# A gate folded into a projection's weights, and the work around the last tile's norm reordered

## The chip, the cores and the metric

The kernel runs on one core of one Trainium2 chip. The metric is the device time of one execution in microseconds (us); of several runs the median counts.

## The reference

One layer of a streaming encoder over 1024 positions and 1024 channels, in float32. Only the middle matters here: two branches (a gated DeltaNet and a banded attention) are each projected and merged by gates; the merged rows go through an output projection, are multiplied by a gate per channel and added to the residual, and are normalised. A second sub-layer follows.

```python
gate_a, gate_b = jnp.split(jax.nn.sigmoid(gates + b_gate[l]), N_BRANCHES, axis=-1)
merged = gate_a * (o_a @ w_branch_a[l]) + gate_b * (o_b @ w_branch_b[l])
mix = merged @ w_o[l]
x = layernorm(DEEPNORM_ALPHA * x + gate_t * mix, ln1_g[l], ln1_b[l])

h = x * (1.0 + scale_f) + shift_f
u = causal_dwconv(h @ w_up[l], conv_ffn[l]) + b_conv_ffn[l]
u_gate, u_val = jnp.split(u, 2, axis=-1)
ffn = (jax.nn.silu(u_gate) * u_val) @ w_down[l]
x = layernorm(DEEPNORM_ALPHA * x + gate_f * ffn, ln2_g[l], ln2_b[l])
```

`gate_t` is a row of 1024 numbers that depends on the conditioning vector alone.

## The kernel before

Every matrix is split into a high and a low part (`split`, L178 and L181: a cast that makes the high part, then a subtraction that makes the low part), and each product is made of three matmuls: high by high, high by low, low by high. The matmuls take 128x512 at a time.

Four stages meet at the place in question. The **branch projections** (`pbr`, L1043) make the merged rows `mh` (high) and `ml` (low; `hh` and `hl` in the profile's names), 128 channels at a time. During the second branch the eight row blocks of `w_o` (k0 to k7) are loaded through the buffers `raw` (three of them) and split into `wo`.

The **output projection** is `mix(t)` (`pwo`, L1107) for eight tiles t of 128 positions, two halves of 512 channels each. For each tile VectorE multiplies the result by the gate row `gtb` (L1135), adds ALPHA times the residual row `r` (L1137 and L1139), and takes statistics (L1081 to L1084); GpSimd raises the variance to the power -1/2 (L1085), VectorE multiplies once more (L1090), and ScalarE normalises (L1093). `store_x1` (L1143, L1144) multiplies the normalised row by `g1b`, adds `b1b`, both on GpSimd for all tiles but one, and writes the row to memory. Eight transposes (`pn`, L1156) turn the tile, and ScalarE applies scale and shift (L1159), out of PSUM.

The **Up stage** (`pup`, L1282) works in a Strassen-like form with seven products for a pair of weight columns. Its operands over positions are blocks: T1 is the difference of the second four tiles and the first four (L1163, then a split), T2 a difference of the halves of the channels (`t2f`, L1170), T3 and T4 further sums (`build`; L1210, L1211, L1215, L1216). Its operands over weights are sums of blocks of `wr` (S1 to S4, L1244, L1247, L1265, L1268), split into `wop`. The first products need only tiles 0 to 3 or the first weights; the others need what comes out of the last tile, t = 7.

The order on each engine is decided by a scheduler when the kernel is built. Each engine then works strictly through its own list, waiting for semaphores; loads and stores stand in one list of the load queue (SP). `tc.issue_after(x)` keeps the scheduler from placing an instruction ahead of x. In the kernel before, all builds of T2 to T4 are held behind `last`, the low half of the last tile's split, and behind the power of the last norm; the store of tile 6 is made with `late`, as is that of tile 7.

Of the kernel before, what the change touches and what calls it, by code (L numbers as in the profile page):

```python
# [154 lines left out]
def hybrid_layer(  # L155
# [873 lines left out]

    wo = []  # L1030
    for br in range(2):
# [4 lines left out]
        for j in range(NK):  # L1036
# [24 lines left out]
            if br == 1 and (j % 2 == 1 or j == NK - 1):  # L1061

                for k in ([j // 2] if j < NK - 1 else range(3, NK)):
                    at_ = MA[2 * k:2 * k + 2] if k < 4 else OB[2 * k - 8:2 * k - 6]
                    a, b = (place(o, [P, D], F32R, "wo") for o in at_)
                    load_split(a, b, w_o2[k * P:k * P + P, :], ACT, DVE)
# [3 lines left out]
    def bcast(key, src):  # L1070
        t_ = ring(key, [P, D])
        SP.dma_start(t_, src.partition_broadcast(P).rearrange("p o n -> p (o n)"))
        return t_
# [53 lines left out]
    for t in range(NT):  # L1127
# [4 lines left out]
        m_ = ring("x1", [P, D])  # L1132
        for n in range(2):
            N = slice(512 * n, 512 * n + 512)
            DVE.tensor_tensor(m_[:, N], ps[n], gtb[:, N], ALU.mult)  # L1135
            if t >= MS:
                DVE.scalar_tensor_tensor(r[:, N], r[:, N], ALPHA, m_[:, N], ALU.mult, ALU.add)  # L1137
        if t < MS:
            DVE.scalar_tensor_tensor(r, r, ALPHA, m_, ALU.mult, ALU.add)  # L1139
        norm(r, r, [slice(0, 512), slice(512, 1024)] if t >= MS else [slice(0, 1024)])  # L1140

        def store_x1(t=t, r=r, m_=m_):
            POOL.tensor_tensor(m_, r, g1b, ALU.mult)  # L1143
            (DVE if t in X1D else POOL).tensor_tensor(m_, m_, b1b, ALU.add)  # L1144
# [2 lines left out]
        if t < X1L:
# [1 line left out]
        else:
            late.append(store_x1)  # L1150
# [425 lines left out]
```

## Time and profile before

| | us |
|---|---|
| median of three runs | 2240.79 |
| lowest, highest | 2235.49, 2244.45 |
| profiled execution | 2240.64 |
| its span | 2238.9 |

The span is the time from the first to the last instruction of the profiled execution. All times of rows are counted from the span's start. In a timeline each row has its start, its duration, engine, line, operation, what is written from what, and in brackets the idle time of the engine just before with the instruction that ended it. The granted clock is the share of full speed that TensorE was given.

### The profile page before, as it was taken

How to read it: one execution, taken by the hardware profiler on the slowest of the kernel's cores; microseconds unless marked ns; L12 is line 12 of the kernel's file. 1: busy time of each engine (PE TensorE's matmuls, PEld its weight loads, DVE VectorE, ACT ScalarE, POOL GpSimd, SP SyncE). 2: the span in 40 equal slices, each digit the busy share in tenths (PEclk: the TensorE clock that was granted, in tenths of full speed). 3: DMA queues.
4: the chain of work that ended last, by engine and by line, in shares of the span. 5: the costliest groups of instructions: out<-in, count | busy, mean ns of one | idle time of the engine just before them, and what ended most of it. 6: DMA issues, size and time to landing. Idle time of an engine off the chain costs nothing.

```text
span 2238.9 us, 31612 instructions
## 1 busy us (share of the span) xinstructions
PE 2129.2 (95%) x11469; PEld 1782.0 (80%) x11469; DVE 1585.5 (71%) x3233; ACT 1025.3 (46%) x2193; POOL 617.0 (28%) x558
## 2 busy tenths in 40 slices
PE   6998999999999999999999999999899999999987
PEld 5687787777878787798989788887688888888875
DVE  8568575765758754567775643458898888889998
ACT  4645243433424334567765642224554444445532
POOL 4323232322323322233432423334110000000064
PEclk9999999999999999999999999999999999999998
DMA  9232333423242412211211523332222222253213
GB/s 284 84 111 73 90 101 105 120 65 117 74 123 80 125 33 98 68 54 47 80 46 59 167 85 128 108 132 94 66 94 85 85 85 85 85 207 110 106 48 131
DMA packets 227263, 220.48 MB, mean 98 GB/s; under 512 B 27354, under 2 KB 184467, under 8 KB 227107
## 3 DMA queue, kind: packets, MB, share of 16 engines
q1 hardware_dynamic: 227027, 218.44, 30.8%
q8 instruction: 90, 1.47, 0.3%
q14 instruction: 66, 0.54, 0.1%
q10 hardware_dynamic: 80, 0.03, 0.0%
HBM read 177.48 MB, written 47.23 MB: 100 GB/s over the span
## 4 chain that ended last, share of the span: by engine, by line
PE 45%; DVE 5%; issue 1%; ACT 1%; POOL 1%; DMA 0%; DVEq 0%; SPq 0%; ACTq 0%; POOLq 0%
PE pup L1282 18%; PE pbr L1043 8%; PE pdn L1460 7%; PE pwo L1107 3%; PE pqk L885 2%; PE pv L900 2%; PE po L975 2%; PE pp L960 1%; PE ps L934 1%; PE pdn L1506 1%; DVE dop L181 0%; DVE hh L1526 0%; DVE hl L181 0%; DMA raw<-in_w_branch_a_dram 0%; DVE G L1163 0%
## 5 line engine op out<-in xcount | busy, mean ns | idle before, releaser
L181 POOL TENSOR_TENSOR wl<-raw,wh 128x1024 fp32r<-128x1024 f32 x88 | 211.4, 2405 | 327.5 <-ACT wh L178 297.9
L1282 PE MATMUL pup<-hh,wop 128*128 128x512 f32 x704 | 229.4, 397 | 5.8 <-ACT SB L1295 3.9
L1282 PE MATMUL pup<-t,wop 128*128 128x512 f32 x792 | 189.9, 393 | 3.9 <-DVE t L181 2.5
L1282 PEld LDWEIGHTS pup<-t,wop 128*128 128x128 f32 x792 | 148.8, 188 | 37.7 <-DVE t L181 2.8
L1282 PEld LDWEIGHTS pup<-hh,wop 128*128 128x128 f32 x704 | 135.0, 192 | 35.4 <-ACT SB L1295 4.3
L178 ACT CAST wh<-raw 128x1024 fp32r<-128x1024 f32 x88 | 92.4, 1050 | 140.1 <-DMA raw<-in_w_in_dram 57.2
L285 PE MATMUL pqkv<-hh,wh 128*128 128x512 f32 x352 | 143.0, 407 | 0.0
L1323 POOL TENSOR_TENSOR cc<-cc,G 128x512 f32<-128x512 f32 x22 | 36.8, 1670 | 378.5 <-DVE G L1305 329.2
L1282 PE MATMUL pup<-hl,wop 128*128 128x512 f32 x352 | 139.9, 398 | 0.9 <-DVE hl L181 0.9
L285 PE MATMUL pqkv<-hl,wh 128*128 128x512 f32 x352 | 140.7, 400 | 0.0
L285 PE MATMUL pqkv<-hh,wl 128*128 128x512 f32 x352 | 139.6, 398 | 0.0
L664 DVE TENSOR_TENSOR FT<-FT,G 128x16 f32<-128x16 f32 (+30 forms) x248 | 120.9, 488 | 19.5 <-POOL G L609 12.2
L178 ACT CAST wop<-wr 128x512 fp32r<-128x512 f32 x110 | 67.1, 621 | 119.7 <-DVE wr L1268 66.5
L945 POOL TENSOR_SCALAR G<-G,FT 128x640 f32<-128x640 f32 (+4 forms) x103 | 69.9, 680 | 183.0 <-DVE FT L944 162.0
L181 DVE TENSOR_TENSOR wop<-wr,wop 128x512 fp32r<-128x512 f32 x110 | 79.5, 731 | 26.2 <-ACT wop L178 25.8
L285 PE MATMUL pgt<-hh,wl 128*128 128x512 f32 x240 | 95.2, 397 | 0.8 <-POOL wl L181 0.8
L285 PE MATMUL pgt<-hh,wh 128*128 128x512 f32 x240 | 95.5, 398 | 0.2 <-DVE tmp L531 0.2
L285 PE MATMUL pgt<-hl,wh 128*128 128x512 f32 x240 | 94.8, 395 | 0.0
L964 DVE TENSOR_TENSOR pl<-pp,ph 128x512 fp32r<-128x512 f32 (+2 forms) x116 | 72.5, 635 | 17.4 <-ACT ph L963 16.6
L1460 PE MATMUL pdn<-hl 128*128 128x512 f32 x324 | 78.0, 394 | 6.1 <-DVE hh L1474 6.1
L1342 DVE SCALAR_TENSOR_TENSOR G<-cc,vt,G 128x1023 f32<-128x1023 f32 (+1 forms) x58 | 75.0, 1297 | 8.1 <-ACT G L1339 8.1
L942 ACT ACTIVATE G<-G,FT 128x640 f32<-128x640 f32 (+4 forms) x103 | 71.6, 695 | 18.9 <-DVE FT L937 16.9
(446 smaller groups left out, 6160.1 us busy)
## 6 DMA issues: line engine op xcount, KB each, us to landing
raw<-in_w_in_dram SPq DMA_DIRECT2D x72, 512.0 KB
wr<-in_w_up_dram SPq DMA_DIRECT2D x44, 512.0 KB
raw<-in_w_ada_dram SPq DMA_DIRECT2D x32, 512.0 KB
dr<-g_d SPq DMA_DIRECT2D x18, 512.0 KB
dr<-in_w_down_dram SPq DMA_DIRECT2D x18, 512.0 KB
wa<-in_w_ada_dram SPq DMA_DIRECT2D x32, 256.0 KB
gates_d<-GT SPq DMA_DIRECT2D x32, 256.0 KB
g_d<-G SPq DMA_DIRECT2D x15, 512.0 KB
```

Source lines behind the costliest of these rows:

```text
L178: ACT.copy(h, src)
L181: return le.tensor_tensor(l, src, f(h), ALU.subtract).ins
L285: PE.matmul(ps, a[:, k, :], r[k][:, 512 * n:512 * n + 512], start=(k == 0 and a is wh and r is rh), stop=(k == NK - 1 and a is wl))
L664: DVE.tensor_tensor(pr[:, :, 0:i + 1], ft[:, :, 0:i + 1], fa[:, i:i + 1, 0:i + 1].to_broadcast([P, 8, i + 1]), ALU.mult)
L942: ACT.activation(sb[:, 0:n], sb[:, 0:n], AF.Exp, bias=mx[:, nb - 1:nb], scale=-1.0, accum_out=mx[:, 2:3])
L945: POOL.tensor_scalar(sb[:, 0:n], sb[:, 0:n], mx[:, 3:4], 0.0, ALU.mult, ALU.add)
L964: DVE.tensor_tensor(pl[:, B, :], pp, f(ph[:, B, :]), ALU.subtract)
L1043: PE.matmul(ps, a[:, k, :], r[k][:, N], start=(k == 0 and a is w[0] and r is rh), stop=(k == NK - 1 and a is w[1]))
L1107: PE.matmul(ps[n], a[:, t, k, :], wo[k][b][:, 512 * n:512 * n + 512], start=(k == 0 and a is mh and b == 0), stop=(k == NK - 1 and a is ml))
L1282: PE.matmul(ps, a[:, u, k, :], b[v][k], start=(new and k == 0 and u == 0 and v == 0), stop=(k == 3 and u == 1), skip_group_check=not new)
L1342: DVE.scalar_tensor_tensor(y[:, d:], cc[:, :S - d], col("conv_f", tap * 44 + ti), y[:, d:], ALU.mult, ALU.add)
L1460: PE.matmul(sets[s_][i], a[:, u, i * P:i * P + P], b[:, v, :], start=(new and j == 0 and u == 0 and v == 0), stop=(j == nq - 1 and u == 1) ...
```

## The change

Five things, as the diff below shows them.

The row `gtb` is now loaded and halved at the start of the second branch projection, and each row block of `w_o` is multiplied by it, on VectorE (L1075 in the changed kernel), before it is split. The multiplication L1135 is gone; the residual step (L1138) adds the PSUM bank itself, half by half, for all tiles. The row blocks are loaded in steps 2, 4, 6 and 7 of eight instead of 1, 3, 5 and 7, to other addresses.

The stores of tiles 6 and 7 have both operations on VectorE. That of tile 6 stands with the tile, that of tile 7 behind the sixth build and behind `last`.

The high part of tiles 0 to 6 is cast on ScalarE, not VectorE.

For the last tile, the first four of eight blocks of T1 are made on VectorE from the transposed tile in PSUM in one step (L1163), with a block `b11` prepared ahead from the merged rows of tile 3 (L1153). ScalarE makes the other four as before.

The builds of T2 to T4 over the first two tiles of each block (t0 = 0) are held only behind the last norm's statistics, or T1, no longer behind `last`, as are the products' weight sums.

```diff
+            if br == 1 and j == 0:
+                gtb = bcast("gtb", mod_d[:, 0:D])
+                DVE.tensor_scalar(gtb, gtb, 0.5, None, ALU.mult)
+            if br == 1 and j and (j % 2 == 0 or j == NK - 1):
+                for k in ([j // 2 - 1] if j < NK - 1 else range(3, NK)):
+                    a, b = (place(o, [P, D], F32R, "wo") for o in (*MA[1:], *OB[:9])[2 * k:2 * k + 2])
+                    raw = W.tile([P, D], F32, tag="raw", bufs=RB, name=nm("raw"))
+                    SP.dma_start(raw, w_o2[k * P:k * P + P, :])
+                    DVE.tensor_tensor(raw, raw, gtb, ALU.mult)
+                    split(a, b, raw, ACT, DVE)
...
-            DVE.tensor_tensor(m_[:, N], ps[n], gtb[:, N], ALU.mult)
-            if t >= MS:
-                DVE.scalar_tensor_tensor(r[:, N], r[:, N], ALPHA, m_[:, N], ALU.mult, ALU.add)
-        if t < MS:
-            DVE.scalar_tensor_tensor(r, r, ALPHA, m_, ALU.mult, ALU.add)
+            DVE.scalar_tensor_tensor(r[:, N], r[:, N], ALPHA, ps[n], ALU.mult, ALU.add)
...
-            POOL.tensor_tensor(m_, r, g1b, ALU.mult)
-            (DVE if t in X1D else POOL).tensor_tensor(m_, m_, b1b, ALU.add)
+            (DVE if t >= X1L else POOL).tensor_tensor(m_, r, g1b, ALU.mult)
+            (DVE if t in X1D or t >= X1L else POOL).tensor_tensor(m_, m_, b1b, ALU.add)
...
+        if t == NT - 1:
+            b11 = place("W8", [P, 4, P], F32, "b11")
+            for q in range(4):
+                DVE.scalar_tensor_tensor(b11[:, q], f(mh[:, 3, q]), b1f[:, q:q + 1], f(ml[:, 3, q]),
+                                         ALU.subtract, ALU.add)
...
+                if t == NT - 1 and g == 0:
+                    mark["t1"] = DVE.scalar_tensor_tensor(
+                        h32[:, q, :], pn[:, k * P:k * P + P], g1f[:, q:q + 1], b11[:, q], ALU.mult, ALU.subtract).ins
+                else:
+                    ACT.activation(h32[:, q, :], pn[:, k * P:k * P + P], AF.Identity,
+                                   bias=b1f[:, q:q + 1], scale=g1f[:, q:q + 1])
...
-            split(mh[:, t], ml[:, t], h32, DVE, DVE)
+            split(mh[:, t], ml[:, t], h32, ACT, DVE)
+            if t >= X1L:
+                store_x1()
+        else:
+            late.append(store_x1)
...
-        with tc.issue_after(mark["norm"] if (t0 + a < TB if TO == 0 else i < TB) else last), tc.issue_after(mark["pow"]):
+        with tc.issue_after(last if t0 else mark["t1" if w == "T4" else "stats"]):
             build(w, t0, a)
+        if i == 5:
+            with tc.issue_after(last):
+                late[0]()
...
-                with tc.issue_after(mark["pow"]) if m in PWM else nullcontext():
+                with tc.issue_after(mark["stats" if m == 5 else "t1"]) if m > 2 else nullcontext():
                     u.product(m)
```

The rest of the diff moves buffers of the Up stage (`yy`, `cc`, `c5`, `u2`) to other addresses.

Three places of the engines' lists show the change. The first is VectorE from the last projection result on (tile 7; `pwo` is its bank, L1244 and L1258 are weight sums, L1081 and L1086 statistics, L1137 and L1138 the residual step). Before:

```order
L1135 TENSOR_TENSOR G_13545<-pwo_14128,gtb_13546 128x512
L1137 SCALAR_TENSOR_TENSOR G_13545<-G_13545 128x512
L1081 BN_STATS ST_12404<-G_13545 128x6
L1244 TENSOR_TENSOR A_1792_14307<-wr_14311 128x512
L181 TENSOR_TENSOR wop_14388<-A_1792_14307,wop_14388 128x512
L1244 TENSOR_TENSOR A_1792_14307<-wr_14315 128x512
L1247 TENSOR_TENSOR A_1792_14307<-A_1792_14307,wr_14310 128x512
L1135 TENSOR_TENSOR G_13545<-pwo_14129,gtb_13546 128x512
L1268 TENSOR_TENSOR wr_14310<-wr_14310,A_1792_14307 128x512
L1265 TENSOR_TENSOR wr_14310<-wr_14310,wr_14311 128x512
L181 TENSOR_TENSOR wop_14406<-A_1792_14307,wop_14406 128x512
L1137 SCALAR_TENSOR_TENSOR G_13545<-G_13545 128x512
```

and now (L1142 and L1143 are the store of tile 6, L1170 the subtraction for tile 6's T1, L1221 and the two rows behind it are builds of T3 and T2):

```order
L1138 SCALAR_TENSOR_TENSOR G_13556<-G_13556,pwo_14131 128x512
L1086 BN_STATS ST_12404<-G_13556 128x6
L1142 TENSOR_TENSOR r_14180<-r_14180,g1b_13557 128x1024
L1088 BN_AGGR ST_12404<-ST_12404 128x2
L1170 TENSOR_TENSOR G_13556<-G_13556,hh 128x512
L1143 TENSOR_TENSOR r_14180<-r_14180,b1b_13559 128x1024
L1089 TENSOR_SCALAR ST_12404<-ST_12404 128x1
L1221 TENSOR_TENSOR SA_14258<-FT_13671,hh 128x512
L181 TENSOR_TENSOR t_1783_14261<-FT_13671,t_1781_14259 128x2x256
L181 TENSOR_TENSOR t_1784_14262<-FT_13671,t_1782_14260 128x2x256
L1258 TENSOR_TENSOR A_1793_14314<-wr_14317 128x512
L1258 TENSOR_TENSOR A_1793_14314<-wr_14321 128x512
```

The gate row is gone, the second residual step stands first, and between the variance (L1089) and the step that needs the power (L1095) stand six operations, the five shown last and one more (L1170); the store of tile 6 has come into the list.

The second place is VectorE around the last tile's T1. Before, from the step behind the power on (L1163 are the two subtractions, L181 on `hl` the low parts of T1):

```order
L1090 SCALAR_TENSOR_TENSOR ST_12404<-ST_12404 128x1
L1244 TENSOR_TENSOR A_1792_14307<-wr_14591 128x512
L1163 TENSOR_TENSOR G_13545<-G_13545,hh 128x512
L1163 TENSOR_TENSOR G_13545<-G_13545,hl 128x512
L1170 TENSOR_TENSOR B_1746_13664<-G_13545 128x512
L181 TENSOR_TENSOR hl<-G_13545,hh 128x512
L1210 TENSOR_TENSOR SA_14254<-FT_13663,hh 128x512
L181 TENSOR_TENSOR t_1782_14257<-FT_13663,t_1780_14255 128x2x256
L181 TENSOR_TENSOR t_1783_14258<-FT_13663,t_1781_14256 128x2x256
L1210 TENSOR_TENSOR SA_14254<-B_1746_13664,hh 128x512
L181 TENSOR_TENSOR hl<-G_13545,hh 128x512
```

and now, from the low part of tile 6 on (L1163 makes T1's first half from the bank `pn`; L1142 is the store of tile 7):

```order
L181 TENSOR_TENSOR hl<-G_13556,hh 128x1024
L181 TENSOR_TENSOR t_1787_14265<-SA_14258,t_1785_14263 128x2x256
L1163 SCALAR_TENSOR_TENSOR G_13556<-pn_14234,aff,b_1777_14229 128x128 x4
L1226 TENSOR_TENSOR FT_13671<-hh,FT_13671 128x2x2x128
L1261 TENSOR_TENSOR A_1793_14314<-A_1793_14314,wr_14316 128x512
L1221 TENSOR_TENSOR SA_14258<-FT_13671,hh 128x512
L1181 TENSOR_TENSOR B_1746_13672<-G_13556 128x512
L181 TENSOR_TENSOR hl<-G_13556,hh 128x512
L1142 TENSOR_TENSOR G_13556<-G_13556,g1b_13557 128x1024
L1227 TENSOR_TENSOR FT_13671<-FT_13671,hl 128x2x2x128
L181 TENSOR_TENSOR hl<-G_13556,hh 128x512
```

The two subtractions have become four operations of 128x128, and a sum, two builds and half of a store stand in front of T1's second low part.

The third place is VectorE where the projection starts; `raw_13523`, `raw_13551` and `raw_13544` are the row blocks k3, k7 and k6, and `wr_14316` is the first Up weight:

```order
L181 TENSOR_TENSOR wop_14325<-wr_14316,wop_14325 128x512
L181 TENSOR_TENSOR wop_14358<-wr_14316,wop_14358 128x512
L1104 TENSOR_SCALAR b1b_13559<-b1b_13559 128x1024
L181 TENSOR_TENSOR hl<-FT_12403,hh 128x4x128
L181 TENSOR_TENSOR wo_13522<-raw_13523,wo_13521 128x1024
L1075 TENSOR_TENSOR raw_13551<-raw_13551,gtb_13035 128x1024
L1123 TENSOR_SCALAR aff<-pmr 128x8
L1124 TENSOR_TENSOR aff<-aff,vt 128x8
L1125 TENSOR_TENSOR aff<-aff,vt 128x8
L1126 TENSOR_TENSOR aff<-pmr,aff 128x8
L181 TENSOR_TENSOR wo_13550<-raw_13551,wo_13549 128x1024
L1075 TENSOR_TENSOR raw_13544<-raw_13544,gtb_13035 128x1024
```

The low parts of the first Up weight stand ahead of k3's low part (`wo_13522`); k7 and k6 are multiplied (L1075) behind it.

## Rows read from the trace of the kernel before

**Rows 1.** The page: TensorE's busy time, its share, its instructions.

```profile
PE 2129.2 (95%) x11469; PEld 1782.0 (80%) x11469; DVE 1585.5 (71%) x3233; ACT 1025.3 (46%) x2193; POOL 617.0 (28%) x558
```

**Rows 2.** Table of windows, busy us of each engine with instructions, clock, DMA share.

```profile
core 0: us, PE busy (x) PEld busy (x) DVE busy (x) ACT busy (x) POOL busy (x), PEclk, DMA share, GB/s
...
1369.00:1456.00 87.00, 87.00 (x383) 71.75 (x383) 36.08 (x36) 21.32 (x27) 33.50 (x21) 1.00 0.31 102
...
1551.00:1580.00 29.00, 18.23 (x63) 13.27 (x61) 24.74 (x36) 15.98 (x34) 10.22 (x5) 0.82 0.15 55
1580.00:1610.00 30.00, 26.65 (x102) 21.16 (x103) 24.77 (x40) 12.03 (x20) 1.61 (x1) 0.89 0.18 53
1610.00:1640.00 30.00, 30.00 (x133) 24.68 (x132) 29.93 (x36) 17.25 (x24) 3.22 (x2) 1.00 0.26 85
```

**Rows 3.** TensorE's timeline at the joint; brackets: idle time before, and its releaser.

```profile
1551.06 0.48 PE L1282 MATMUL pup<-hh,wop 128*128 128x512 f32 x1
...
1560.67 0.80 PE L1282 MATMUL pup<-hh,wop 128*128 128x512 f32 x1 [3.91 <-ACT SB L1295]
...
1569.68 1.97 PE L1156 MATMUL pn<-ident,G 128*128 128x128 f32 x8 [3.57 <-ACT G L1093]
...
1576.83 0.73 PE L1282 MATMUL pup<-hh,wop 128*128 128x512 f32 x2 [1.85 <-ACT hh L178]
...
1579.15 0.50 PE L1282 MATMUL pup<-t,wop 128*128 128x512 f32 x1 [1.02 <-ACT wop L178]
1580.59 0.80 PE L1282 MATMUL pup<-hl,wop 128*128 128x512 f32 x1 [0.94 <-DVE hl L181]
...
1598.31 1.88 PE L1282 MATMUL pup<-t,wop 128*128 128x512 f32 x7 [2.45 <-DVE t L181]
```

**Rows 4.** VectorE's timeline at the joint.

```profile
1549.06 2.85 DVE L1137 SCALAR_TENSOR_TENSOR G<-G 128x512 f32<-128x512 f32 x1
...
1552.55 2.16 DVE L1244 TENSOR_TENSOR A<-wr 128x512 f32<-128x512 f32 x1
...
1557.21 0.69 DVE L1135 TENSOR_TENSOR G<-pwo,gtb 128x512 f32<-128x512 f32 x1
1557.81 0.68 DVE L1268 TENSOR_TENSOR wr<-wr,A 128x512 f32<-128x512 f32 x1
...
1566.36 1.22 DVE L181 TENSOR_TENSOR hl<-G,hh 128x1024 fp32r<-128x1024 f32 x1
1567.49 0.69 DVE L181 TENSOR_TENSOR wop<-wr,wop 128x512 fp32r<-128x512 f32 x1
...
1569.86 0.69 DVE L1244 TENSOR_TENSOR A<-wr 128x512 f32<-128x512 f32 x1 [1.08 <-DMA wr<-in_w_up_dram]
...
1573.36 2.76 DVE L1163 TENSOR_TENSOR G<-G,hl 128x512 f32<-128x512 f32 x1
...
1579.85 0.69 DVE L181 TENSOR_TENSOR hl<-G,hh 128x512 fp32r<-128x512 f32 x1
```

**Rows 5.** GpSimd's timeline at the joint.

```profile
1548.98 2.38 POOL L1143 TENSOR_TENSOR G<-r,g1b 128x1024 f32<-128x1024 f32 x1 [1.96 <-ACT r L1093]
...
1566.52 2.06 POOL L1085 TENSOR_TENSOR ST<-ST,mhalf 128x1 f32<-128x1 f32 x1 [12.37 <-DVE ST L1084]
```

**Rows 6.** Groups of instructions by line, VectorE, 1456 to 1600, and one line.

```profile
L1135 DVE TENSOR_TENSOR G<-pwo,gtb 128x512 f32<-128x512 f32 x16 | 10.4, 683 | 3.5 <-PE pwo L1107 3.5
...
L727 DVE SCALAR_TENSOR_TENSOR vs<-pks,SM,vs x56: 330/350/352, 209.7 to 920.5; 128x128 f32<-128x128 f32 x56
```

**Rows 7.** Timelines of the load queue (SP) and of ScalarE at the mix's start.

```profile
1454.95 0.33 SPq L186 DMA_DIRECT2D raw<-in_w_o_dram  x1
...
1457.64 0.45 SPq L1238 DMA_DIRECT2D wr<-in_w_up_dram  x1
...
1566.41 0.38 SPq L1238 DMA_DIRECT2D wr<-in_w_up_dram  x1
...
1460.23 1.05 ACT L178 CAST wo<-raw 128x1024 fp32r<-128x1024 f32 x1 [6.00 <-DMA raw<-in_w_o_dram]
...
1467.30 1.15 ACT L178 CAST wop<-wr 128x512 fp32r<-128x512 f32 x2 [5.50 <-DMA wr<-in_w_up_dram]
```

More of the change, by code (lines that the diff above doesn't have):

```diff
@@ L105 @@
     "gb": _at("GB", 512, 2), "macc": _at("M", 0, 1),
-    "st": _at("ST", 12, 2), "mv": _at("ST", 4, 4, 36), "gtb": (_E1[0],), "g1b": (_E1[1],),
+    "st": _at("ST", 12, 2), "mv": _at("ST", 4, 4, 36), "gtb": (MA[0],), "g1b": (_E1[1],),
     "b1b": (_E1[2],), "r": (_E1[3], ("GL", 0)), "x1": _at("GL", 1024, 2, 1024),
@@ L1028, in hybrid_layer, with bcast @@
         load_split(oahk[k], oalk[k], oa_d[k], ACT, POOL if k in OL else DVE)
+    def bcast(key, src):
+        t_ = ring(key, [P, D])
+        SP.dma_start(t_, src.partition_broadcast(P).rearrange("p o n -> p (o n)"))
+        return t_
     wo = []
@@ L1060, in hybrid_layer @@
                     load_split(obh[k], obl[k], ob_d[k], ACT, DVE)
[L1061 to L1066, printed above, removed]
+            if br == 1 and j == 0:
[8 more added lines that the diff above has]
+                    split(a, b, raw, ACT, DVE)
                     wo.append((a, b))
[L1070 to L1073, printed above, removed]
     mark = {}
@@ L1131, in hybrid_layer @@
         SP.dma_start(r, x2[t * P:t * P + P, :])
[L1132 removed]
+        m_ = ring("x1", [P, D]) if t < X1L else r
         for n in range(2):
             N = slice(512 * n, 512 * n + 512)
[L1135 to L1139 removed]
+            DVE.scalar_tensor_tensor(r[:, N], r[:, N], ALPHA, ps[n], ALU.mult, ALU.add)
         norm(r, r, [slice(0, 512), slice(512, 1024)] if t >= MS else [slice(0, 1024)])
         def store_x1(t=t, r=r, m_=m_):
[L1143 to L1144 removed]
+            (DVE if t >= X1L else POOL).tensor_tensor(m_, r, g1b, ALU.mult)
+            (DVE if t in X1D or t >= X1L else POOL).tensor_tensor(m_, m_, b1b, ALU.add)
             SP.dma_start(x1_d[t], m_)
[L1147 removed]
+        if t < NT - 1 and t < X1L:
             store_x1()
[L1149 to L1150 removed]
         h32 = ring("h2", [P, NK, P])
+        if t == NT - 1:
[3 more added lines that the diff above has]
+                                         ALU.subtract, ALU.add)
         for g in range(2):
@@ L1158, in hybrid_layer @@
                 q = 4 * g + k
-                ACT.activation(h32[:, q, :], pn[:, k * P:k * P + P], AF.Identity,
-                               bias=b1f[:, q:q + 1], scale=g1f[:, q:q + 1])
-            if t >= 4 and g == 0:
+                if t == NT - 1 and g == 0:
[4 more added lines that the diff above has]
+                                   bias=b1f[:, q:q + 1], scale=g1f[:, q:q + 1])
+            if 4 <= t < NT - 1 and g == 0:
                 for part in (mh, ml):
@@ L1361, in hybrid_layer @@
         u.finish()
-        for fn in late:
-            with tc.issue_after(mark["pow"]) if PWL else nullcontext():
-                fn()
-        late = []
     for p in range(2, NP):
```

7 lines of the change are left out of this document (2 added, 5 removed).

## The prediction

> **What bounds the kernel now.** The page comes first: TensorE is busy for 2129.2 us, 95% of the span [rows 1], so a change can only pay where TensorE waits or runs slowly. The second reading is the table of windows around the place that the diff touches. In the two windows 1551 to 1580 and 1580 to 1610 TensorE is busy for 18.23 of 29 and 26.65 of 30 us and its mean granted clock is 0.82 and 0.89 [rows 2]; from 1610 on it is full at a clock of 1.00. This is the joint between the output projection and the Up stage: the last tile must be normalised, transposed and split before most Up products have an operand.
>
> The third reading is TensorE's timeline there [rows 3]. The first Up matmul starts at 1551.06; the 104th starts at 1598.31, behind the last wait. Seven matmuls from there take 1.88 us, which is 0.23 from start to start. So 103 matmuls and eight transposes are 24.6 us of work in 47.25 us: 22.6 us are lost. The rows name 13.74 us of idle time (3.91, 3.57, 1.85, 1.02, 0.94, 2.45). The other 9 us or so are mostly matmuls at the half level of the clock: the rows that follow the 3.91 and the 0.94 show single matmuls of 0.80 us, against 0.50 where the clock was up. The releasers are ScalarE four times and VectorE twice.
>
> The fourth reading asks who is late behind these releasers, on VectorE [rows 4]. The projection's last matmul is done at 1550.4, but the gate multiplication of the last half tile (L1135) starts only at 1557.21. Ahead of it stand a residual step of 2.85 us (L1137) and a weight sum of 2.16 us (L1244), forms that otherwise take 0.69; GpSimd runs the store of tile 6 at the same time, from 1548.98 [rows 5]. The last subtraction of T1 shows the same once more, 2.76 us at 1573.36. GpSimd then sits idle for 12.37 us until the variance arrives, because statistics and sums stand in turn in one queue. The low half of T1 starts at 1579.85, 29 us behind the last projection matmul. So VectorE's queue bounds the joint, by its length, its order and its collisions with GpSimd.
>
> **The change, part by part.**
>
> *Gate into the weights.* Eight VectorE products of 128x1024 (1.22 us each by the subtraction of the same size at 1566.36, 1.13 to the start of the next [rows 4]) are added, some 9 to 10 us, under the branch projections and the first two mix tiles. TensorE is busy there throughout and VectorE for 36.08 of 87 us [rows 2], so I cost them at nothing. In exchange 16 multiplications by the gate (0.683 us [rows 6]) go, two of them in the joint: 1.2 us at the 0.60 from start to start that 1557.21 and 1557.81 show.
>
> What this puts at risk is the start of the mix. In the new order k3's split stands, on ScalarE and VectorE, behind casts of the first Up weight. Before, row block k7 was issued second in a burst of loads, behind g1b, and was there at 1460.23; the first Up weight was issued seventh, at 1457.64, and was there at 1467.30, five turns of 1.4 us later [rows 7]. Now that weight is the second of the burst, so it should be there at about 1460.2. Going down the order with these durations: b1b one turn later, k3's high part done at 1463.0, low at 1464.2. TensorE has 36 matmuls of k0 to k2 of two tiles first, 8.2 us from 1456.3, and needs k3 at 1464.5 and 1465.4. k6 takes k3's buffer: issued 1464.2, landed 4.5 us later (a load by itself took 3.45, issued 1566.41 [rows 7] and awaited until 1569.86 [rows 4]; k7 in the burst 5.28: I take the middle), multiplied 1470.1, high part 1471.2, low 1472.4, needed 1472.8 and 1473.8. The margins are 1.2 to 1.6 us: no wait, price 0; at 5.28 it is still 0.6.
>
> *Stores of tiles 6 and 7 to VectorE.* Four operations of 1.13, 4.5 us more on VectorE. The collisions go: 2.16 (L1137), 1.47 (L1244) and 2.07 (L1163), together 5.7 us of VectorE's time.
>
> *T1 of the last tile from the bank.* Four 128x128 operations (0.26 to 0.35 each, by the nearest row, of the same form out of PSUM, 0.350 [rows 6]) replace four activations on ScalarE and two 512-wide subtractions. Four others of the same price prepare b11 ahead, under the mix, where nothing waits for them. VectorE gives 1.2 for 1.0 to 1.4: even. But T1's first half needs no ScalarE any more, which works on the second half beside it.
>
> *Casts to ScalarE, sums and halves of T2 to T4 reordered.* The last 1024-wide cast (0.6) leaves VectorE's joint. The rest is order: between the last projection result and the variance's return now stand operations that were due anyway.
>
> **The sum.** Since VectorE bounds the joint, I count its work in the new order, from the last projection result (1550.4) to the low weight operand of the 118th Up matmul, the last that I find waiting. It is 55 operations 512 wide at 0.60 (33.0), five 1024 wide at 1.13 (5.65), four of 128 at 0.35 (1.4) and three tiny ones (0.3): 40.35 us, which ends at 1590.8. Before, that matmul ran 14 behind the last wait, at 1598.31 + 14 x 0.23 = 1601.5. So 10.7 us if VectorE never waits. The bounds: with 0.26 for the 128-wide ones and no wait 11.2. On the other side, GpSimd's power step took 2.06 us [rows 5] and each low part must follow its ScalarE cast, so some waits stay; 0 to 5 us, and I take 0.9, as six operations are placed over the power step. TensorE itself still waits, by this replay, 2.8 us for T1's low half (about 1569.0, 11 us earlier than before) and 3 to 5 us at about 1582 for another weight operand, but it catches up in front of the 118th with a microsecond to spare. Behind it the order gives TensorE one unbroken stream, as before. Gain 10.7 - 0.9 = 9.8: from the profiled execution's 2240.64 to **2230.8**. That execution lies 0.15 us under the median of the runs, so nothing is added. Elsewhere (the buffers of yy, cc, c5 and u2, and a few neighbours exchanged at the seam to the Down stage) I find no wait changed: 0, with 1 us either way.
>
> The Trainium skill ("TensorE: Matmul & The Clock Gate", section "HAM oscillation") warns that an array left idle falls to half its clock, and that only sustained work brings it back. The trace agrees for the waits of 3.91 and 3.57 us; behind the 2.45 the matmuls ran at full speed. It is a rival below.
>
> **The rivals.**
>
> *VectorE's floor is met and the seam gives a little.* No wait on VectorE gives 11.2, and a microsecond at the seam to the Down stage 12.2: 2228.4 to 2229.4. For it: the queue is always full. Against: every low part hangs on a cast.
>
> *The clock falls again.* TensorE's wait at 1582 is longer than the 2.45 us that did no harm. If the half level then holds, 33 matmuls up to the 118th take twice 0.23: it gets there at 1582.2 + 15.2 = 1597.4, a gain of 4.1, **2236.5**. Against it: in the window from 1580 the mean of 0.89 over 30 us [rows 2] says that the half level lasted 6.6 us in all, about 14 matmuls: 3.2 us more, in front of the 118th at 1593.0 and a gain of 8.5.
>
> *The wait only moves.* VectorE was busy for 24.74 of 29 us from 1551 to 1580 [rows 2], so 4.3 idle, 1.08 of it for the load at 1569.86. If it idles as long in the new joint, behind casts and GpSimd's power step, the gain is 10.7 - 4.3 = 6.4: **2234.2**. For it: each low part follows its cast on another engine. Against: the new order puts three to six other operations between.
>
> *The first Up weight lands late* (the other side). If its load still lands at 1467.3 as before, VectorE's FIFO holds k3's low part until about 1471.7, 6.3 us behind TensorE's need at 1465.4, and the clock falls behind that wait, another 4.4 (half of the joint's loss to the clock). The loss of 10.7 exceeds the gain: **2241.5**. It decides as soon as the load lands later than about 1466.5; up to 1461.4 it costs nothing. For it: the queue order; against: the issue order moved it from the end of the burst to its second place.
>
> **How the numbers follow.** A measurement of this kernel tells about 0.5%, 11.2 us, from no change; faster means below 2229.6. Chances: forecast 0.42 (own range 2229 to 2233), floor met 0.27, clock 0.12, wait moved 0.12, late weight 0.07. Range: from 2227 (floor, seam, and a microsecond of spread between runs) to 2237 (which takes in the clock and the moved wait); what lies outside is the late weight and a few hundredths on each side. Faster: 0.27 and a sixth of the forecast, 0.34. Slower by over 0.5% would need the late weight with further stalls, 0.05. Same: 0.61.
>
> **What would show it.** Right: mix continuous from 1456 to 1550; no store on GpSimd in the joint and no VectorE operation of 2 us or more there; the last gate row gone and the residual step within 1 us of the last projection matmul; T1's low half near 1569; the 118th Up matmul near 1591. Wrong: a TensorE wait between 1464 and 1474 for k3 or k6; half-speed matmuls between 1582 and 1591; VectorE idle for several microseconds in the joint; or a new wait behind the 118th matmul, where VectorE is now only just ahead.

## The result, and the profile after

The changed kernel takes 2230.05 us (median of eight runs, 2223.45 to 2233.05); the kernel before takes 2239.43 (eight runs, 2235.49 to 2245.62). The ratio is 0.9947 with a 95% interval from 0.9936 to 0.9958. The medians differ by 9.4 us; the interval stands for 9.4 to 14.3 us less. The forecast was 2230.8, a gain of 9.8.

The runs of one kernel differ by up to 10 us, as much as the whole effect. Most of that lies ahead of the change: in the profiled executions of this study the projection began anywhere from 1453.1 to 1460.8 us, with the same program up to 1369. The stages behind it move far less: in all fourteen profiles the projection took 93.6 to 93.8 us, and the Up stage from its 141st matmul on 389.6 to 389.9. So I compare stages, taken from the first and the last matmul of each. These are the rows of the Up matmuls by line, of before and of the changed kernel (shortest, median and longest in ns, first and last start):

```profile
L1282 PE MATMUL pup<-hh,wop x704: 388/390/796, 1551.1 to 1996.5; 128*128 128x512 f32 x176
```

```profile
L1296 PE MATMUL pup<-hh,wop x704: 388/389/628, 1554.0 to 1990.5; 128*128 128x512 f32 x176
```

| stage (us) | before | changed |
|---|---|---|
| projection, first to last matmul | 93.8 | 93.6 |
| Up, first to last matmul | 445.5 | 436.5 |
| from the last Up matmul to the span's end | 242.4 | 240.8 |

The Up stage gives 9.0 us, and what follows 1.6. (The expectations below have 445.4 for before, from the rounded rows.) All of the 9.0 lies ahead of the 141st Up matmul. Up to there TensorE's waits fell from 14.1 to 8.7 us. What matmuls at half the clock (the half level) cost it fell from 5.8 to 3.1; that is an estimate from the starts of the matmuls: where two follow each other without an idle time and more than 0.35 us apart, I count what exceeds 0.23. The changed kernel's profiled execution began its projection 3.1 us later than that of before (1459.4 against 1456.3), so its rows lie about 3 us later in the span up to the joint.

The windows of the changed kernel, in the columns of [rows 2]:

```profile
core 0: us, PE busy (x) PEld busy (x) DVE busy (x) ACT busy (x) POOL busy (x), PEclk, DMA share, GB/s
...
1551.00:1580.00 29.00, 24.86 (x106) 19.03 (x104) 26.58 (x45) 17.48 (x36) 0.93 (x1) 0.94 0.19 62
1580.00:1610.00 30.00, 25.50 (x104) 20.17 (x103) 28.46 (x43) 15.56 (x23) 3.01 (x2) 0.94 0.27 81
1610.00:1640.00 30.00, 30.00 (x133) 24.66 (x132) 29.97 (x38) 15.33 (x21) 1.62 (x1) 1.00 0.27 88
```

In the window from 1551, in which the joint lies 3 us later than before, TensorE is busy 24.86 us where it was 18.23, at a granted clock of 0.94 instead of 0.82. Its timeline, answering to [rows 3]:

```profile
1467.89 1.66 PE L1110 MATMUL pwo<-wo,hh 128*128 128x512 f32 x6
...
1553.98 0.48 PE L1296 MATMUL pup<-hh,wop 128*128 128x512 f32 x1
...
1563.32 1.36 PE L1159 MATMUL pn<-ident,G 128*128 128x128 f32 x8 [0.92 <-ACT G L1098]
...
1567.85 1.03 PE L1296 MATMUL pup<-hh,wop 128*128 128x512 f32 x2 [0.39 <-ACT hh L178]
1569.89 0.50 PE L1296 MATMUL pup<-t,wop 128*128 128x512 f32 x1 [1.01 <-ACT t L178]
1572.13 0.50 PE L1296 MATMUL pup<-hl,wop 128*128 128x512 f32 x1 [1.74 <-DVE hl L181]
...
1585.31 4.36 PE L1296 MATMUL pup<-t,wop 128*128 128x512 f32 x11 [3.27 <-DVE wop L181]
...
1594.82 0.50 PE L1296 MATMUL pup<-t,wop 128*128 128x512 f32 x1 [1.23 <-ACT t L178]
...
1595.62 0.62 PE L1296 MATMUL pup<-hh,wop 128*128 128x512 f32 x2
```

The waits of 3.91 and 3.57 us have become nothing and 0.92. What is left is 8.6 us in six waits, the longest one 3.27. The last row holds the 118th Up matmul. VectorE's timeline, answering to [rows 4, 6]:

```profile
1466.31 1.22 DVE L181 TENSOR_TENSOR wo<-raw,wo 128x1024 fp32r<-128x1024 f32 x1
...
1553.39 0.69 DVE L1138 SCALAR_TENSOR_TENSOR G<-G,pwo 128x512 f32<-128x512 f32 x1 [3.10 <-PE pwo L1110]
...
1554.72 1.21 DVE L1142 TENSOR_TENSOR r<-r,g1b 128x1024 f32<-128x1024 f32 x1
...
1557.66 0.15 DVE L1089 TENSOR_SCALAR ST<-ST 128x1 f32<-128x1 f32 x1
...
1561.33 0.15 DVE L1095 SCALAR_TENSOR_TENSOR ST<-ST 128x1 f32<-128x1 f32 x1
...
1565.61 1.12 DVE L1163 SCALAR_TENSOR_TENSOR G<-pn,aff,b 128x128 f32<-128x128 f32 x4
...
1571.39 0.68 DVE L181 TENSOR_TENSOR hl<-G,hh 128x512 fp32r<-128x512 f32 x1
...
1584.57 0.68 DVE L181 TENSOR_TENSOR wop<-A,wop 128x512 fp32r<-128x512 f32 x1
...
1593.63 0.69 DVE L1343 TENSOR_TENSOR cc<-pup,G 128x512 f32<-128x512 f32 x1 [1.17 <-PE pup L1296]
1594.28 0.69 DVE L181 TENSOR_TENSOR wop<-A,wop 128x512 fp32r<-128x512 f32 x1
```

The residual step starts 0.4 us behind the last projection matmul (1552.96), the step behind the power (L1095) 8.4 us behind it; before it was 18.6. T1's last low half starts at 1571.39, in before's time about 1568.4, against 1579.85. No operation is longer than its shape asks for. GpSimd has only the power left in the joint (answering to [rows 5]):

```profile
1557.88 0.93 POOL L1090 TENSOR_TENSOR ST<-ST,mhalf 128x1 f32<-128x1 f32 x1 [13.95 <-DVE ST L1089]
```

At the start of the mix, ScalarE's rows answer to [rows 7]:

```profile
1463.24 1.14 ACT L178 CAST wop<-wr 128x512 fp32r<-128x512 f32 x2 [4.34 <-DMA wr<-in_w_up_dram]
...
1464.81 1.05 ACT L178 CAST wo<-raw 128x1024 fp32r<-128x1024 f32 x1
```

The first Up weight is there at 1463.24, k3's high part at 1465.86, its low part (VectorE's row at 1466.31) at 1467.53, and TensorE takes k3 at 1467.89 without a wait.

### The profile page after: what moved, and what is told of

The parts are those of the page before. It is cut to its first block, busy times and chain, and to the rows that moved or that the text cites. A ratio compares the mean times of both kernels' runs of the same rounds, so it can differ in the third digit from the quotient of the medians.

```text
span 2231.3 us, 31605 instructions
## 1 busy us (share of the span) xinstructions
PE 2129.5 (95%) x11469; PEld 1781.7 (80%) x11469; DVE 1575.9 (71%) x3234; ACT 1032.8 (46%) x2196; POOL 607.2 (27%) x554
## 4 chain that ended last, share of the span: by engine, by line
PE 45%; DVE 6%; issue 1%; ACT 1%; DMA 0%; POOL 0%; DVEq 0%; SPq 0%; ACTq 0%
PE pup L1296 18%; PE pbr L1048 8%; PE pdn L1470 6%; PE pwo L1110 4%; PE pqk L885 2%; PE pv L900 2%; PE po L975 2%; PE pp L960 1%; PE ps L934 1%; DVE hh L1536 0%; DVE hh L1507 0%; DMA raw<-in_w_branch_a_dram 0%; DVE dop L181 0%; DVE hl L181 0%; DVE hh L1506 0%
## 5 line engine op out<-in xcount | busy, mean ns | idle before, releaser
L181 POOL TENSOR_TENSOR wl<-raw,wh 128x1024 fp32r<-128x1024 f32 x88 | 211.7, 2408 | 325.1 <-ACT wh L178 295.6
L664 DVE TENSOR_TENSOR FT<-FT,G 128x16 f32<-128x16 f32 (+30 forms) x248 | 120.7, 487 | 19.5 <-POOL G L609 12.2
L1337 POOL TENSOR_TENSOR cc<-cc,G 128x512 f32<-128x512 f32 x15 | 26.2, 1751 | 265.7 <-DVE G L1319 222.7
L181 DVE TENSOR_TENSOR wop<-wr,wop 128x512 fp32r<-128x512 f32 x110 | 80.7, 740 | 25.1 <-ACT wop L178 25.0
L1296 PEld LDWEIGHTS pup<-hl,wop 128*128 128x128 f32 x352 | 66.6, 189 | 16.2 <-DVE hl L181 2.1
```

What stands on the lines that cost most here:

```text
L181: return le.tensor_tensor(l, src, f(h), ALU.subtract).ins
L664: DVE.tensor_tensor(pr[:, :, 0:i + 1], ft[:, :, 0:i + 1], fa[:, i:i + 1, 0:i + 1].to_broadcast([P, 8, i + 1]), ALU.mult)
L1296: PE.matmul(ps, a[:, u, k, :], b[v][k], start=(new and k == 0 and u == 0 and v == 0), stop=(k == 3 and u == 1), skip_group_check=not new)
```

## The experiments

Every run was timed in five rounds beside the kernel before. The last four columns come from its profile: the Up stage; how long behind the start of the last projection matmul the step behind the power of the last norm starts (call it the norm step); and, up to the 141st Up matmul, TensorE's waits and the cost of the half level, as above.

| kernel | median us | ratio to before, 95% | Up stage | norm step | waits | half level |
|---|---|---|---|---|---|---|
| before | | | 445.5 | 18.6 | 14.1 | 5.8 |
| changed | 2230.05 | 0.9936 to 0.9958 | 436.5 | 8.4 | 8.7 | 3.1 |
| e1 stores on GpSimd | 2232.97 | 0.9945 to 0.9973 | 439.7 | 10.1 | 10.2 | 4.2 |
| e2 order of before | 2234.66 | 0.9957 to 0.9981 | 438.7 | 10.0 | 12.2 | 1.7 |
| e3 gate in the joint | 2233.17 | 0.9950 to 0.9976 | 436.1 | 9.8 | 8.5 | 2.7 |
| e4 stores late | 2222.18 | 0.9907 to 0.9931 | 431.3 | 5.8 | 5.4 | 2.1 |
| e5 T1 by ScalarE | 2229.24 | 0.9933 to 0.9960 | 435.2 | 8.4 | 8.7 | 1.9 |
| e6 addresses only | 2239.06 | 0.9983 to 1.0004 | 446.1 | 18.6 | 14.2 | 6.4 |
| e7 fold only | 2232.89 | 0.9948 to 0.9976 | 439.3 | 8.6 | 12.3 | 2.4 |
| e8 stores and T4 late | 2226.23 | 0.9917 to 0.9946 | 431.8 | 5.8 | 4.2 | 3.3 |
| e9 order only | 2234.33 | 0.9959 to 0.9984 | 439.1 | 11.0 | 10.8 | 3.8 |
| e10 stores only | 2239.87 | 0.9983 to 1.0004 | 444.3 | 16.2 | 14.7 | 4.7 |
| e11 late, T1 by ScalarE | 2229.46 | 0.9930 to 0.9969 | 434.2 | 5.8 | 6.9 | 3.3 |
| e12 casts on VectorE | 2229.06 | 0.9924 to 0.9967 | 435.3 | 8.4 | 6.7 | 2.7 |

e1 to e5, e8, e11 and e12 start from the changed kernel, e6, e7, e9 and e10 from the kernel before. There is one profile of each kernel, so how far an Up stage repeats is not shown; e6, whose edit hardly touches the joint, lies 0.6 us from before. Of the kernels made from the changed one only e4 has an interval of the time that is clear of the changed kernel's; differences of a microsecond or two between the others rest on the stages alone.

**e1, stores of tiles 6 and 7 on GpSimd.**

```diff
-            (DVE if t >= X1L else POOL).tensor_tensor(m_, r, g1b, ALU.mult)
-            (DVE if t in X1D or t >= X1L else POOL).tensor_tensor(m_, m_, b1b, ALU.add)
+            POOL.tensor_tensor(m_, r, g1b, ALU.mult)
+            (DVE if t in X1D else POOL).tensor_tensor(m_, m_, b1b, ALU.add)
```

> The changed kernel with both operations of the stores of tiles 6 and 7 back on GpSimd, at their new places in the program. Measure: from the first to the last Up matmul (before 445.4 us, changed 436.5). If the collisions of VectorE with GpSimd cost what the rows of before show (5.7 us of VectorE's time), VectorE loses 4.5 us of work and gains 5.7 of blocking: about 437.7, total 2231 (0 to 3 us above the changed kernel), and VectorE operations of 2 us and more are back in the joint. Rival, the collisions fall on operations that nobody waits for: the 4.5 us of work come off the joint, about 432, total 2226.

439.7: the collisions cost more than expected, 3.2 us net. The four stretched rows below are 8.0 us longer than their forms take otherwise; less the 4.5 us of work that left the list, that makes 3.5. VectorE's timeline of e1 and below it GpSimd's:

```profile
1548.90 2.16 DVE L1221 TENSOR_TENSOR SA<-FT,hh 128x512 f32<-128x512 f32 x1
1550.98 3.48 DVE L181 TENSOR_TENSOR t<-FT,t 128x512 fp32r<-128x512 f32 x2
...
1560.70 2.90 DVE L1222 TENSOR_TENSOR SA<-SA,hl 128x512 f32<-128x512 f32 x1
1563.53 3.37 DVE L181 TENSOR_TENSOR hl<-G,hh 128x1024 fp32r<-128x1024 f32 x1
```

```profile
1548.11 2.40 POOL L1142 TENSOR_TENSOR r<-r,g1b 128x1024 f32<-128x1024 f32 x1 [10.43 <-issue]
...
1560.68 2.38 POOL L1142 TENSOR_TENSOR G<-G,g1b 128x1024 f32<-128x1024 f32 x1 [6.77 <-ACT cc L1340]
```

Single operations of 0.68 to 1.22 take 2.16 to 3.37 us, and a pair 3.48 instead of 1.29, while GpSimd works on a store. The rival is out.

**e2, the holds of before.**

```diff
-        with tc.issue_after(last if t0 else mark["t1" if w == "T4" else "stats"]):
+        with tc.issue_after(last), tc.issue_after(mark["pow"]):
             build(w, t0, a)
...
-                with tc.issue_after(mark["stats" if m == 5 else "t1"]) if m > 2 else nullcontext():
-                    u.product(m)
+                u.product(m)
...
+        for fn in late:
+            fn()
```

> The changed kernel with the holds of the kernel before: all builds of T2 to T4 behind the last low half of T1 and the power, products without a hold, tile 7's store after the first Up pair. If the order carries a good part of the gain, as VectorE cannot work ahead while the last norm runs: Up stage 440 to 443 us (changed 436.5, before 445.4), total 2234 to 2237, with idle time on VectorE before the step behind the power. Rival, only the length of VectorE's list counts: 436 to 437, total 2230.

438.7, 2.2 above the changed kernel: the direction was right, the size was half. The norm step came at 10.0, hardly later than with the holds, and the fold alone puts it there too (e7). VectorE did stand idle ahead of it, for 1.64 us, but for a weight's load.

**e3, the gate row back in the joint.**

```diff
-                    DVE.tensor_tensor(raw, raw, gtb, ALU.mult)
...
-            DVE.scalar_tensor_tensor(r[:, N], r[:, N], ALPHA, ps[n], ALU.mult, ALU.add)
+            DVE.tensor_tensor(q_[:, N], ps[n], gtb[:, N], ALU.mult)
+            DVE.scalar_tensor_tensor(r[:, N], r[:, N], ALPHA, q_[:, N], ALU.mult, ALU.add)
```

> The changed kernel without the gate in the weights: the product with the gate row is back before each residual step, and the eight products on the rows of the weights are gone. Mine: two operations of 0.6 us come back into the joint, Up stage 437 to 438 us (changed 436.5), total 2231 to 2232, mix unbroken in both. Rival, the folding carries most of the gain, because the norm chains of all tiles run on time: Up stage above 440, total 2235 or more.

436.1: neither. With the rest of the change in place the fold is worth nothing in the Up stage. The median is 3 us above the changed kernel's, with intervals that overlap; the stages don't show where 3 us would lie.

**e4, both stores behind the last build of T4.**

```diff
-            if t >= X1L:
-                store_x1()
-        else:
+        if t >= X1L:
             late.append(store_x1)
...
-        if i == 5:
-            with tc.issue_after(last):
-                late[0]()
+    with tc.issue_after(mark["t4"]):
+        for fn in late:
+            fn()
```

> The changed kernel with the stores of tiles 6 and 7 held on VectorE until the last build of T4 is done, so four operations of 1.13 us leave the part of VectorE's list on which the joint's matmuls wait; three others of 0.6 move ahead. If VectorE's list bounds the joint: Up stage 433 to 434 us (changed 436.5), total 2227 to 2228. Rival, the waits of the second half of the joint hang on buffers and casts between TensorE and ScalarE: 436 to 436.5, total 2230. Bad end: the held stores delay rows of the Up stage that VectorE owes at once, 437 to 439.

431.3, 2222.18 us: 5.2 us off the Up stage, a little more than the 4.5 that the operations weigh. TensorE's waits in the joint of e4, three where the changed kernel has six:

```profile
1562.32 1.02 PE L1294 MATMUL pup<-hh,wop 128*128 128x512 f32 x2 [2.32 <-ACT hh L178]
1563.87 0.51 PE L1294 MATMUL pup<-t,wop 128*128 128x512 f32 x1 [0.53 <-ACT t L178]
1566.94 0.79 PE L1294 MATMUL pup<-hl,wop 128*128 128x512 f32 x1 [2.56 <-DVE hl L181]
```

This version beats both kernels: its interval, 0.9907 to 0.9931, ends below that of the changed kernel.

**e5, T1 by ScalarE.**

```diff
...
-                if t == NT - 1 and g == 0:
-                    mark["t1"] = DVE.scalar_tensor_tensor(h32[:, q, :], pn[:, k * P:k * P + P], ...
-                else:
-                    ACT.activation(...)
+                ACT.activation(...)
...
+            if t >= 4 and g == 0:
                 for part in (mh, ml):
+                    mark["t1"] = DVE.tensor_tensor(h32[:, G4], h32[:, G4], f(part[:, t - 4, G4]), ALU.subtract).ins
```

> The changed kernel with the last tile's T1 made as before: eight activations on ScalarE and two subtractions 512 wide on VectorE, no b11; the holds that named T1 now name the last subtraction. Mine: VectorE's work is even, but T1's low half comes some 1.5 us later, and VectorE fills that with other work: Up stage 436.5 to 438 us (changed 436.5), total 2230 to 2232. Rival, T1's road through ScalarE was what the joint waited for: 439.5 or more, total 2233 or more.

435.2, 1.3 us less. T1's low half did come later, 22.5 us behind the last projection matmul instead of 18.4, but VectorE filled the time and the later waits shrank: TensorE's waits add up to 8.7 us in both kernels. What is less is the half level, 1.9 us instead of 3.1. So T1's road made no difference to the sum of the waits, and nearly all of the 1.3 us lies in the clock.

**e6, addresses only.**

```diff
-"cc": ("B0", "B1", "B2"),
-"yy": ("B3", ("GF", 0), ("GF", 1024)), "c5": _at("GF", 512, 2, 2048), "u2": _at("GF", 512, 2, 3072),
+"cc": ("B0", ("GL", 1024), "B1"),
+"yy": ("B3", "B2", ("GL", 0)), "c5": _at("GL", 512, 2, 3072), "u2": _at("GL", 512, 2, 2048),
```

> The kernel before with nothing changed but the addresses of yy, cc, c5 and u2 (and the last two stores called ahead of the Up pair, as the addresses need it). The Down stage and what follows it took 242.2 us before and 240.6 in the changed kernel. If the new addresses are the cause, they take 240.6 here, with an Up stage of 445 to 446, total about 1.6 us under before. Rival, the seam's new neighbours come from the joint's other timing and the list order: 242.2 here, total as before.

From the first Down matmul on it took 240.6 us, as in the changed kernel (before 242.2), with an Up stage of 446.1. But the addresses are not all of these 1.6 us. Up to the 701st Down matmul the four kernels with the old addresses (before, e7, e9, e10) take 160.2 us and the ten with the new ones 159.3: that is 0.9. The other 0.7 goes with the clock. Behind the wait in front of the 761st Down matmul TensorE ran at a granted clock of 0.79 over 8 us in before, and in e8 and e11, which have the new addresses; in e6 and the ten others it was 1.00. Rows of before, e6 and e8:

```profile
2178.95 1.75 PE L1460 MATMUL pdn<-hl 128*128 128x512 f32 x6 [2.34 <-DVE hh L1474]
2180.50 2.76 PE L1460 MATMUL pdn<-dop,hl 128*128 128x512 f32 x6
```

```profile
2177.67 1.66 PE L1457 MATMUL pdn<-hl 128*128 128x512 f32 x6 [2.13 <-DVE hh L1471]
2179.16 1.52 PE L1457 MATMUL pdn<-dop,hl 128*128 128x512 f32 x6
```

```profile
2165.84 1.69 PE L1468 MATMUL pdn<-hl 128*128 128x512 f32 x6 [2.34 <-DVE hh L1482]
2167.35 2.74 PE L1468 MATMUL pdn<-dop,hl 128*128 128x512 f32 x6
```

The second row's six matmuls take 2.76 and 2.74 us, or 1.52. So e7, e9 and e10 are at 241.4 to 241.5 with the old addresses, e8 and e11 at 241.3 to 241.4 with the new ones. In the kernel's time (0.9983 to 1.0004) e6 cannot be told from no change.

**e7, the fold only,** in the kernel before:

```diff
...
+                    DVE.tensor_tensor(raw, raw, gtb, ALU.mult)
+                    split(a, b, raw, ACT, DVE)
...
-            DVE.tensor_tensor(m_[:, N], ps[n], gtb[:, N], ALU.mult)
-            if t >= MS:
-                DVE.scalar_tensor_tensor(r[:, N], r[:, N], ALPHA, m_[:, N], ALU.mult, ALU.add)
+            DVE.scalar_tensor_tensor(r[:, N], r[:, N], ALPHA, ps[n], ALU.mult, ALU.add)
```

> The kernel before with only the gate folded into the weights (loads, eight products, residual step from the bank); stores, T1, casts, holds and addresses as before. Mine: two operations leave the joint and the last residual step moves up a little, the collisions stay: Up stage 443 to 445 us (before 445.4), mix 93.6 to 93.7 without a wait, total 0 to 2 us under before. Rival, the folding carries the gain: 440 or less, total 5 us or more under before. Bad end: k3 or k6 late, mix of 95 or more.

439.3: the rival was right, 6.2 us from an edit whose two operations in the joint weigh 1.2. VectorE's timeline of e7, with the last projection matmul at 1550.1:

```profile
1554.06 0.68 DVE L1138 SCALAR_TENSOR_TENSOR G<-G,pwo 128x512 f32<-128x512 f32 x1
...
1556.70 0.15 DVE L1089 TENSOR_SCALAR ST<-ST 128x1 f32<-128x1 f32 x1
...
1558.70 0.15 DVE L1095 SCALAR_TENSOR_TENSOR ST<-ST 128x1 f32<-128x1 f32 x1
```

The residual step starts at 1554.06, the norm step at 1558.70. The whole chain moved forward in VectorE's list: with one step less, the scheduler put the statistics ahead of weight sums that had stood in front of them.

**e8, T4's builds late as well** (on top of e4's edit).

```diff
-        with tc.issue_after(last if t0 else mark["t1" if w == "T4" else "stats"]):
+        with tc.issue_after(last if t0 or w == "T4" else mark["stats"]):
```

> As e4 (both stores behind the last build of T4), and in addition all builds of T4 behind T1's last low half. In e4 TensorE waited 2.56 us for that low half, before which VectorE did two subtractions and two additions of T4. If VectorE's order is still what is left: the wait falls to under 1.5 us, Up stage 429 to 430.5 us (e4 431.3), total 1 to 2 us under e4. Rival, its list is so full that the builds only come back in front of the next wait: 431 to 432, total as e4.

431.8, the rival's number, but not by the rival's mechanism: no wait came back further on. The wait for the low half fell from 2.56 to 1.67 us, and the waits together from 5.4 to 4.2. TensorE lost as much to the clock. In the 12 us from the 49th Up matmul on it has 26 matmuls in either kernel, busy for 8.88 us at a granted clock of 0.72 in e4, and for 10.09 us at 0.58 here:

```profile
1566.82 1.31 PE L1294 MATMUL pup<-hh,wop 128*128 128x512 f32 x2 [2.33 <-ACT hh L178]
...
1570.84 0.80 PE L1294 MATMUL pup<-hl,wop 128*128 128x512 f32 x1 [1.67 <-DVE hl L181]
```

**e9, the holds only,** in the kernel before (the diff of e2 the other way round, with GpSimd's stores left where they were):

> The kernel before with only the holds of the change (builds over the first tiles and weight sums held behind statistics or T1 instead of the last low half and nothing); gate row, GpSimd's stores, T1 and casts as before. The gate folded alone brought the Up stage from 445.4 to 439.3 us, and the changed kernel without the fold lost nothing; in all kernels with a short joint the step behind the power came 6 to 10 us after the last projection matmul, in the kernel before 18.6. If the place of this norm chain in VectorE's list is the cause, and not the gate's two operations, the holds alone do the same: the step behind the power at 9 to 11, Up stage 438 to 441, total 4 to 7 us under before, although the gate row is still there. Rival, the fold itself is needed: Up stage 443 or more.

439.1, as expected: the gate row, GpSimd's stores and T1 as before, and 6.3 us are gone. VectorE's timeline of e9 (last projection matmul at 1548.3), and GpSimd's row of tile 7's store:

```profile
1550.80 0.67 DVE L1135 TENSOR_TENSOR G<-pwo,gtb 128x512 f32<-128x512 f32 x1
...
1554.93 0.15 DVE L1084 TENSOR_SCALAR ST<-ST 128x1 f32<-128x1 f32 x1
...
1559.21 0.15 DVE L1090 SCALAR_TENSOR_TENSOR ST<-ST 128x1 f32<-128x1 f32 x1
...
1568.24 0.68 DVE L1170 TENSOR_TENSOR B<-G 128x512 f32<-128x512 f32 x1
```

```profile
1560.99 10.13 POOL L1143 TENSOR_TENSOR G<-G,g1b 128x1024 f32<-128x1024 f32 x1 [4.91 <-ACT G L1093]
```

The gate row starts 2.5 us behind the last projection matmul instead of 7.2, the norm step 11.0. The collisions are not quite the same: three operations are stretched by 4.0 us in all, where before four lost 5.9.

**e10, the stores only,** in the kernel before:

```diff
+            (DVE if t >= X1L else POOL).tensor_tensor(m_, r, g1b, ALU.mult)
+            (DVE if t in X1D or t >= X1L else POOL).tensor_tensor(m_, m_, b1b, ALU.add)
...
```

> The kernel before with only the stores of tiles 6 and 7 on VectorE, at the change's places. The norm chain stays behind the weight sums in VectorE's list. If the chain's place is the cause: the collisions go (5.7 us of VectorE's time), 4.5 us of work come, Up stage 444 to 446.5 us (before 445.4), total as before, step behind the power still at 16 us or more. Rival, the collisions are what made the chain late: step behind the power at 12 or less, Up stage under 442.

444.3. The collisions are gone, and the norm step still starts at 1567.69, 16.2 us behind the last projection matmul:

```profile
1565.37 0.15 DVE L1084 TENSOR_SCALAR ST<-ST 128x1 f32<-128x1 f32 x1
...
1567.69 0.16 DVE L1090 SCALAR_TENSOR_TENSOR ST<-ST 128x1 f32<-128x1 f32 x1 [0.44 <-POOL ST L1085]
```

So the collisions were not the main thing that made the chain late: without them it starts 2.4 us earlier, with the two operations of tile 6's store now ahead of it.

**e11, e4 with T1 by ScalarE** (the diffs of e4 and e5 together):

> As e4 (both stores behind the last build of T4), with T1 by ScalarE as in e5, which had been 1.3 us shorter than the changed kernel in the Up stage. If the two add: Up stage 430 us (e4 431.3), total 1 us under e4, 2221 to 2224. Rival, T1 through ScalarE now ends last, since VectorE has less ahead of it: 432 to 434.

434.2, 2.9 above e4: the rival. TensorE waits 4.17 us for T1's high part here, against 2.32 in e4. About half of the 2.9 are waits (6.9 against 5.4 us), the rest is nearly all half level (3.3 against 2.1). T1 from the bank saves waits only where the stores are out of VectorE's way; with them in the list (e5) it saved none.

**e12, the casts of tiles 0 to 6 on VectorE.**

```diff
-            split(mh[:, t], ml[:, t], h32, ACT, DVE)
+            split(mh[:, t], ml[:, t], h32, DVE, DVE)
```

> The changed kernel with the high parts of tiles 0 to 6 cast on VectorE as before. Mine: one cast of 0.6 us stands in the joint's list on VectorE, ScalarE has one of 1.05 less: Up stage 436.5 to 437.5 us (changed 436.5), total within 1 us of the changed kernel. Rival, ScalarE's list is what the joint waits for at its first half (four of six waits of the kernel before were put down to it): 435 or less.

435.3, 1.2 below the changed kernel: nearer to the rival. Which of ScalarE's casts it shortened I did not separate; the order of both lists shifts with it.

## Why the prediction was right

*The bound, VectorE's list in the joint:* right. From the residual step at 1553.39 to the end of the 118th matmul's weight operand at 1594.97 are 41.6 us, of which VectorE stood idle for 1.2 (row 1593.63). That is 40.4 us of work, where the sum had 40.35. Taking work out of this list (e4) shortens the Up stage by what it weighs and a little more; making it collide (e1) lengthens it. TensorE's two waits came where they were forecast: 1.74 us for T1's low half, up to 1569.2 in before's time (forecast 2.8, about 1569.0), and 3.27 us for a weight operand, up to 1582.4 (3 to 5, about 1582).

*The wait left on VectorE:* taken as 0.9, was 1.17, but behind another cause than the power step or a cast. The power came 0.93 us after its call and was hidden by the six operations. VectorE (row 1593.63 above) and ScalarE waited for the same Up matmul, the 114th, which ends at 1593.59; ScalarE's two casts then kept TensorE waiting for 1.23. TensorE's row and ScalarE's:

```profile
1593.20 0.39 PE L1296 MATMUL pup<-hh,wop 128*128 128x512 f32 x1
```

```profile
1593.63 0.62 ACT L178 CAST wop<-A 128x512 fp32r<-128x512 f32 x1 [5.33 <-PE pup L1296]
1594.15 0.61 ACT L178 CAST t<-SA 128x512 fp32r<-128x512 f32 x1
```

That matmul was late by the clock. Its start stands 27 starts and 7.89 us behind the wait of 3.27; at 0.23 each they would have taken 6.2. By this estimate it would have ended at 1591.9, before VectorE had come to the row that waited (1592.47). So the term was nearly of the right size by luck: it was put down to the power and the casts, and the clock took it. The 118th matmul stands at 1595.62, 2.9 us to be taken off for the later start: 1592.7, forecast 1591.7. The clock rival, with the half level for 14 matmuls only, had 1593.0. In the Up stage 9.0 us against 9.8.

*The mix:* right in each row. With 3.1 us taken off for the later start, the first Up weight was there at 1460.2 (forecast 1460.2), k3's parts at 1462.8 and 1464.5 (1463.0, 1464.2), k6 issued at 1464.5 (1464.2). The late weight did not happen.

*The seam to the Down stage:* taken as 0 with 1 either way, was 1.6: 0.9 from the addresses, 0.7 from the clock in the Down stage (e6), which e8 and e11 lost with the new addresses as well. The two small errors, 0.8 less and 1.6 more, nearly cancel, and that is luck.

*Single terms do not hold by themselves.* The gate row's two operations (1.2 us) are worth 0 with the rest of the change (e3) and 6.2 without it (e7). The stores were priced at a net gain of 1.2 (5.7 less 4.5); alone they give 1.2 (e10), with the rest of the change 3.2 (e1). T1 from the bank was priced even, and in the waits it is (e5). The sum came out because it was made over the list as a whole, not from these terms.

*Length, order and collisions were named side by side; the runs rank them.* All kernels near 445 have the norm step at 16 us or later, all at 440 or less have it at 11 or earlier. The fold alone (e7) or the holds alone (e9) bring it there, and each gives two thirds of the gain; the second of them then adds little (e2, e3). Removing collisions without moving the chain gives 1.2, net of the 4.5 us of work that the stores bring onto VectorE (e10). So the first two thirds are for the most part order, and length and collisions decide about the rest. That is not a clean cut: e7 also takes 1.2 us of work out, e9 also has 1.9 us less of collisions, and part of every gain is the clock's (table).

*The rivals.* VectorE's idle time did not move along (1.2 us, not 4.3), and the floor was not quite met. *The clock* held in part, and the sign named for it, half-speed matmuls between 1582 and 1591, was there. Behind the 3.27 us wait eleven matmuls take 4.36 us at a granted clock of 0.61, with seven starts 0.43 apart. It did not last up to the 118th, but VectorE's wait of 1.17 us goes back to it. By the Trainium skill ("TensorE: Matmul & The Clock Gate", section "HAM oscillation") an idle array loses half its clock; the trace agrees here, where it did not for the 2.45 us wait of before. The length of one wait does not tell by itself: behind 0.39, 1.01 and 1.74 us in close order the granted clock was 0.55 from 1572.13 to 1575.90.

## What to carry to other kernels

Where one engine's list bounds a stretch, add up that list from the last input to the last operand that somebody waits for: the sum over the list holds where prices of single edits do not, since two edits that both bring a chain forward pay only once. Look at how far the chain that everything hangs on starts behind its input, and what the scheduler placed ahead of it; work that nobody waits for (here a store) belongs behind the stretch, not on another engine inside it. Where runs differ by as much as the effect, compare stages by their first and last matmul, and look at the granted clock before putting a microsecond down to an edit: what e8 gained in waits and what e5 seemed to gain went by the clock.

## What was not expected of the hardware

GpSimd's multiplication of 128x1024 in e9 took 10.13 us (1560.99 to 1571.12) where other rows of it show 2.4 to 3.2. VectorE worked from its list without a gap until 1568.92, its operations at their usual length; GpSimd was done 2.2 us behind that. In e1 it went the other way: three VectorE operations and one of a pair were stretched by 1.5 to 2.2 us each. The Trainium skill ("SBUF — State Buffer", section "Who interferes with whom") says that a VectorE operation with two inputs in SBUF and a GpSimd operation that reads SBUF exclude each other, and that the one that starts first holds the port for the whole instruction. The rows of e1 agree. That a full VectorE list can keep GpSimd out for eight microseconds goes beyond it, and rests on this one row.
